# Recurrence halves in groups of four, and a gate moved from the weights to the projected result

## The chip, the cores and the metric

The kernel runs on one core of a Trainium2 chip, as one program. The metric is device time in microseconds of one execution. Three executions were timed, and a further one was taken by the hardware profiler; the rows below are from that one.

The engines are named as in the profile: PE is TensorE's matmul, PEld its weight load, DVE is VectorE, ACT ScalarE, POOL GpSimd, SP SyncE. PEclk is the granted clock of TensorE as a share of full speed.

## The reference, cut to what matters

One block of a mixed network on 1024 tokens of width 1024. What the change touches is the second branch (a gated linear recurrence), the merge of both branches, and the output projection with its residual gate `gt1`:

```python
def rglru_branch(xb, gb, conv_w, conv_b, w_rgate, b_rgate, w_igate, b_igate, lam):
    xc = conv(xb, conv_w) + conv_b                      # causal, width 4
    gate_r = sigmoid(blockdiag(xc, w_rgate) + b_rgate)
    gate_i = sigmoid(blockdiag(xc, w_igate) + b_igate)
    log_a = -8.0 * gate_r * softplus(-lam)
    a = exp(log_a)
    u = sqrt(-expm1(2.0 * log_a)) * (gate_i * xc)
    h = associative_scan(a, u)                          # h[t] = a[t] h[t-1] + u[t]
    return h * gelu(gb)
...
merged = (sigmoid(proj[..., o3:o4]) * (y_a @ p_a) + sigmoid(proj[..., o4:]) * (y_b @ p_b))
x = x + gt1[:, None, :] * (merged @ w_out)
h2 = modulate(rmsnorm(x, g_ffn), sh2, sc2)
x = x + gt2[:, None, :] * hier_moe(h2, ...)
```

`gt1` is one row of 1024 numbers, worked out from the condition `c`; it multiplies the columns of `merged @ w_out`.

## The kernel before, in words

The program is written once, without a loop on the device. A list scheduler sets the order on each engine when the program is built: among the instructions whose inputs and buffers it takes to be ready it issues the one that was written first. So a later line can be issued before an earlier one, but on the chip each engine then works through its list in order, and an instruction that waits holds up those behind it. SP issues nearly all DMAs, in one such list. Pools hand out buffers by name, with a fixed number each (`bufs`); a tile waits until the one that had its buffer is done with.

Products are made in pairs of a rounded value and its remainder: a weight `raw` is cast on ACT to `wh` (L216), the remainder `wl = raw - wh` is made on DVE (L217), and a product is `wh` by `yh`, `wh` by `yl` and `wl` by `yh`, three matmuls of 128 x 512 for each block of 128 inputs.

The stages around the change, in order of time in the profiled execution:

1. Up to 842.7 us: branch a and the projections into gates (`gd`), recurrence inputs (`xcd`, `ggd`) and branch a's result (`yad`), all in DRAM. The last store of `yad` is L643, the last gate halves are L769 and L770.
2. To 924.6: branch a's result is read in eight halves and split (L792 to L798, raw buffers of two). Then L878 to L880 run eight times: `lru(b, hf)` and `merge(0, n)`. `lru` takes one block `b` of 128 channels and half of the tokens: two gate matmuls (L833), two tanh on ACT (L834), exp (L837), tanh (L838) and sqrt (L839) on ACT, five operations and a scan (L844) on DVE, of which L840 needs the gates alone and the others the root; the result is cast on ACT (L849) and its remainder made on POOL (L850). The second half of a block takes the last column of the first. The scales of exp and tanh come from a short series on DVE in `lam` (L806 to L821). `merge(0, n)` multiplies branch a's result by a block of its weights: 24 matmuls in two PSUM banks of four, each then multiplied by its gate on DVE (L868). It does not use the recurrence's result.
3. To 989.2: `merge(1, d)` for eight blocks `d`, 24 matmuls each over the recurrence's result (`yh[4..7]`, `yl[4..7]`), DVE (L870), POOL (L871), ACT (L872) and DVE (L874) on each half. After each one, two pieces of the output weights of 128 x 512 are loaded, multiplied by `gt1` on POOL (L915), cast on ACT (L917) and their remainder made on DVE (L918): eight pieces of the first half of the output columns in the first four blocks, eight of the second half in the others.
4. From then to about 1107: the output projection, first the left half of the columns for eight tiles of 128 tokens (`hf == 0`, 24 matmuls a tile), then the right half. DVE adds each to `x1` (L1107), ACT squares it (L1108). In the right half each finished tile is transposed and multiplied by the router's weights, normalised and written to DRAM as `h2` (L1119 to L1126). The loads of `x` (L1072) and of three rows go out ahead of the first half, the first eight expert weights of 512 KB (`issue(8)`, L1095) with the second.

`x1` takes the place of `ybs`, in which the recurrence's result lies, so `x` is loaded once the last merges have read that. The output weights lie in 16 buffers `w` that the expert weights use after them.

Of the kernel before, what the change touches and what calls it, by code (L numbers as in the profile page):

```python
# [92 lines left out]
def _build(tc, A, out, dump, stop, top):  # L93
# [3 lines left out]
    def dmp(name, ap, idx=slice(None)):  # L97
        if name in dump:
            Y.dma_start(dump[name][idx], ap)
# [523 lines left out]
    def rwkv_finish(q):  # L623
        pd, hf, rk, yt = (q[n] for n in ("pd", "hf", "rk", "yt"))
        p, vs, g2 = pd["p"], pd["vs"], pd["g2"]
        tsl = slice(hf * 512, hf * 512 + 512)
        dmp("wkv", yt, (p, slice(None), tsl))

        yo = tmp.tile([128, 512], F32, name="u")
        S.activation(yo, yt, AF.Square)  # L630
        pss = psum.tile([128, 4, 2], F32, name="u1")
        for j in range(4):
            T.matmul(pss[:, j], yo[:, j * 128:j * 128 + 128], bo64[:, 0:128:64], start=True, stop=True)
        pin = inv_bcast(pss, GN_EPS)
        V.scalar_tensor_tensor(yt, yt, col("lnx_g", p), pin.rearrange("p j t -> p (j t)"), op0=OP.mult, op1=OP.mult)
        pb = psum.tile([128, 512], F32, name="u1")
        T.matmul(pb, bo, rk, start=True, stop=True)
        V.tensor_mul(rk, pb, vs[:, tsl])
        V.scalar_tensor_tensor(yo, yt, col("lnx_b", p), rk, op0=OP.add, op1=OP.add)
        pg = psum.tile([128, 512], F32, name="u2")  # L640
        T.matmul(pg, g2, sg[:, tsl], start=True, stop=True)
        V.tensor_mul(yo, yo, pg)
        Y.dma_start(yad[p][:, tsl], yo)  # L643
        dmp("y_a", yo, (p, slice(None), tsl))


# [174 lines left out]
    V.tensor_scalar(sp[:, 5], sp[:, 5], 2.0, None, op0=OP.mult)  # L821
    prev = {}

    def lru(b, hf):
        sl = slice(hf * 512, hf * 512 + 512)
        xc, gg = half("xc"), half("gg")
        Y.dma_start(xc, xcd[b][:, sl])
        Y.dma_start(gg, ggd[b][:, sl])
        dmp("xc", xc, (b, slice(None), sl))
        gr, gi = half("gr"), half("gi")  # L830
        for i, (dst, bias) in enumerate(((gr, "brh"), (gi, "bih"))):
            pg = psum.tile([128, 512], F32, name="pt", bufs=2)
            T.matmul(pg, wbd[:, b, i], xc, start=True, stop=True)  # L833
            S.activation(dst, pg, AF.Tanh, scale=0.5, bias=dcol[bias][:, b:b + 1])  # L834

        rc = half("rc")
        S.activation(rc, gr, AF.Exp, scale=sp[:, 0, b:b + 1], bias=sp[:, 0, b:b + 1])  # L837
        S.activation(gr, gr, AF.Tanh, scale=sp[:, 5, b:b + 1], bias=sp[:, 5, b:b + 1])  # L838
        S.activation(gr, gr, AF.Sqrt)  # L839
        V.scalar_tensor_tensor(gi, gi, 1.0, xc, op0=OP.add, op1=OP.mult)  # L840
        V.scalar_tensor_tensor(gr, rc, 1.0, gr, op0=OP.add, op1=OP.mult)
        V.tensor_mul(gr, gr, gi)
        hs_ = half("hs")
        V.tensor_tensor_scan(hs_, rc, gr, prev[b][:, 511:512] if hf else 0.0, op0=OP.mult, op1=OP.add)  # L844
        prev[b] = hs_
# [5 lines left out]


    def merge(i, d):
        raw = wpool.tile([128, 512], F32, name="wr", bufs=2)
        Y.dma_start(raw, A["pab"][i, d])
        wh, wl = split_w(raw, wpool)
        for hf in range(2):
# [17 lines left out]
                                       op1=OP.subtract)  # L875
                dmp("merged", g, (d, slice(None), sl))

    for n in range(8):  # L878
        lru(n // 2, n % 2)
        merge(0, n)  # L880
    gs_.close()
    yas.close()
    if stop == "lru":
# [18 lines left out]
    V.tensor_scalar(tri, rel, 0.0, None, op0=OP.is_gt)  # L902
    onb = rpc.tile([128, 128], BF, name="onb")
    V.memset(onb, 1.0)

    gt1 = wpool.tile([128, 1024], F32, name="gt1", bufs=1)
    load_row(gt1, 0)
    oh_, ol_ = {}, {}
    for d in range(8):
        merge(1, d)  # L910
        for kk in (2 * d, 2 * d + 1):
            hf, k = divmod(kk, 8)
            raw = wpool.tile([128, 512], F32, name="wo", bufs=2)
            Y.dma_start(raw, A["wout"][:, k, hf * 512:hf * 512 + 512])
            P.tensor_mul(raw, raw, gt1[:, hf * 512:hf * 512 + 512])  # L915
            h, l = (lambda t: (t[:, 0], t[:, 1]))(wo.tile([128, 2, 512], F32R, name="w", bufs=NRAW))
            S.copy(h, raw)  # L917
            V.tensor_sub(l, raw, h.bitcast(F32))  # L918
            oh_[k, hf], ol_[k, hf] = h, l
    m2.close()  # L920
    rp = rps.enter_context(pool("rp", 1, side="right"))
    if stop == "merged":
# [137 lines left out]
    with pool("xt", 1) as xt:  # L1060
        for i, n in enumerate(MODS[1:3]):
            mrow[n] = xt.tile([128, 1024], F32, name="m_" + n)
            load_row(mrow[n], i + 1)
        gf_ = xt.tile([128, 1024], F32, name="h2", bufs=2)
        Y.dma_start(gf_, A["grow"][0:1].to_broadcast([128, 1024]))
        V.scalar_tensor_tensor(mrow["sc2"], mrow["sc2"], 1.0, gf_, op0=OP.add, op1=OP.mult)
        for n in MODS[1:3]:
# [24 lines left out]
        for hf in range(2):  # L1092
            sl = slice(hf * 512, hf * 512 + 512)
            if hf:
                issue(8)  # L1095
            for t in range(8):
                tsl = slice(t * 128, t * 128 + 128)
                xv = x1[:, t]
# [4 lines left out]
                for k in range(8):  # L1103
                    T.matmul(ps, mh[k][:, tsl], oh_[k, hf], start=(k == 0), stop=False)
                    T.matmul(ps, mh[k][:, tsl], ol_[k, hf], start=False, stop=False)
                    T.matmul(ps, ml[k, t // 4][:, t % 4 * 128:t % 4 * 128 + 128], oh_[k, hf], start=False, stop=(k == 7))  # L1106
                V.tensor_add(xv[:, sl], xv[:, sl], ps)  # L1107
                S.activation(ps, xv[:, sl], AF.Square, accum_out=ssx[:, t, hf:hf + 1])  # L1108
                if hf == 0:
                    continue  # L1110
# [5 lines left out]
                pl2 = psum.tile([128, 36], F32, name="pl", bufs=2)  # L1116
                T.transpose(pl2, lgT, ident[0:36, 0:36])
                V.scalar_tensor_tensor(LG[:, t], pl2, y, br, op0=OP.mult, op1=OP.add)
                h2 = xt.tile([128, 1024], F32, name="h2", bufs=2)  # L1119
                if t == 7:  # L1120
                    choose(xt, 5, 8)
                for i in range(2):
# [371 lines left out]
```

## Time and profile before

| | us |
|---|---|
| median of 3 runs | 1537.52 |
| lowest and highest | 1531.68, 1541.69 |
| profiled execution, its own time | 1536.43 |
| its span, first to last instruction | 1534.5 |
| PE busy in the span | 1326.4 (86%) |
| DVE, ACT, POOL busy | 920.1, 490.3, 408.1 |
| mean granted TensorE clock | 0.945 |

Matmuls are pipelined and their ends are modelled, so two that follow at once overlap in the records, and the time that one takes off the engine is read from the distance of their starts. A number in brackets behind an instruction is the engine's idle time ahead of it, and who ended it. The chain of work that ended last is PE for 60% of the span and DVE for 20%.

### The profile page before, as it was taken

What the parts mean: (1) busy time and instruction counts of PE and PEld (TensorE: products, weight loads), DVE (VectorE), ACT (ScalarE), POOL (GpSimd) and SP (SyncE); (2) the same over time, 40 slices, a digit from 0 to 9 for tenths busy, and PEclk for the clock granted to TensorE, in tenths of its full rate; (3) what the DMA queues carried; (4) which work ended last, traced back from release to release, by engine and by line L of the source; (5) the groups of instructions that cost most, each with busy time, mean ns of one, the idle gap of its engine ahead of it and who ended that gap; (6) DMA issues with size and microseconds to landing.
All of it is one profiled execution on the core that took longest, in us unless ns stands there. A gap on an engine that the chain in (4) does not pass through costs nothing.

```text
span 1534.5 us, 23186 instructions
## 1 busy us (share of the span) xinstructions
PE 1326.4 (86%) x8524; PEld 926.5 (60%) x8524; DVE 920.1 (60%) x2073; ACT 490.3 (32%) x900; POOL 408.1 (27%) x327
## 2 busy tenths in 40 slices
PE   1898998899999999999999797899759899999910
PEld 0686765666766667766766475687545555755500
DVE  8936868687658562475433577614775435625557
ACT  3222323132222222231211693312424424514321
POOL 7001212121101110111111326601314434634514
PEclk9998999999999999999999899999969999999965
DMA  6333432333433211112211754541448979979952
GB/s 262 130 117 138 126 110 92 99 99 115 151 131 94 66 57 35 51 57 60 63 42 35 238 167 150 187 163 56 165 165 299 385 281 402 349 267 393 349 234 100
DMA packets 113403, 248.59 MB, mean 162 GB/s; under 512 B 39632, under 2 KB 40960, under 8 KB 112256
## 3 DMA queue, kind: packets, MB, share of 16 engines
q1 hardware_dynamic: 105952, 230.22, 42.7%
q0 software_dynamic: 7328, 16.79, 3.0%
q8 instruction: 69, 1.13, 0.3%
q14 instruction: 54, 0.44, 0.1%
HBM read 218.16 MB, written 38.36 MB: 167 GB/s over the span
## 4 chain that ended last, share of the span: by engine, by line
PE 60%; DVE 20%; DMA 9%; ACT 4%; issue 4%; POOL 2%; POOLq 0%; SPq 0%; DVEq 0%; ACTq 0%
PE pg L319 5%; PE pg L318 5%; PE pg L320 5%; DMA xg<-h2d,gidx 3%; DMA w<-in_we 3%; PE ph L1372 3%; PE pj L318 2%; DVE wa L228 2%; PE pj L320 2%; PE pj L319 2%; PE st L603 2%; PE ph L1315 2%; PE st L617 2%; PE pj L1106 2%; PE ph L1317 2%
## 5 line engine op out<-in xcount | busy, mean ns | idle before, releaser
L318 PE MATMUL pg<-hh,wh 128*128 128x512 f32 x376 | 158.9, 423 | 8.4 <-DVE cr L680 5.0
L319 PE MATMUL pg<-hl,wh 128*128 128x512 f32 x376 | 157.2, 418 | 0.0
L320 PE MATMUL pg<-hh,wl 128*128 128x512 f32 x376 | 155.9, 415 | 0.0
L560 POOL TENSOR_TENSOR WV<-VT,m 128x512 f32<-128x512 f32 x32 | 35.5, 1110 | 369.5 <-PE st L603 280.3
L1282 ACT CAST wh<-w 128x1024 fp32r<-128x1024 f32 x96 | 98.5, 1053 | 82.1 <-DMA w<-in_we 30.7
L1283 DVE TENSOR_TENSOR wl<-w,wh 128x1024 fp32r<-128x1024 f32 x68 | 92.0, 1376 | 36.1 <-ACT wh L1282 33.7
L228 DVE SCALAR_TENSOR_TENSOR wa<-wa,cb 128x1024 f32<-128x1024 f32 x64 | 79.6, 1251 | 27.1 <-DMA wa<-in_wada 27.0
L318 PEld LDWEIGHTS pg<-hh,wh 128*128 128x128 f32 x376 | 72.3, 192 | 33.3 <-issue 9.4
L216 ACT CAST wh<-wr 128x512 fp32r<-128x512 f32 x88 | 54.4, 619 | 100.0 <-PE pj L319 50.4
L217 DVE TENSOR_TENSOR wl<-wr,wh 128x512 fp32r<-128x512 f32 x72 | 53.5, 742 | 50.7 <-ACT wh L216 50.4
L319 PEld LDWEIGHTS pg<-hl,wh 128*128 128x128 f32 x376 | 72.3, 192 | 17.7 <-issue 4.7
L320 PEld LDWEIGHTS pg<-hh,wl 128*128 128x128 f32 x376 | 71.9, 191 | 17.2 <-issue 4.0
L610 DVE SCALAR_TENSOR_TENSOR St<-St,Dc,st 128x64 f32<-128x64 f32 x128 | 35.4, 277 | 76.4 <-PE st L608 76.3
L318 PE MATMUL pj<-hh,wh 128*128 128x512 f32 x192 | 77.5, 404 | 3.2 <-DVE carry L365 3.2
L1283 POOL TENSOR_TENSOR wl<-w,wh 128x1024 fp32r<-128x1024 f32 x28 | 71.0, 2541 | 30.6 <-ACT wh L1282 23.1
L320 PE MATMUL pj<-hh,wl 128*128 128x512 f32 x192 | 76.9, 401 | 0.0
L319 PE MATMUL pj<-hl,wh 128*128 128x512 f32 x192 | 75.8, 395 | 0.0
L1315 PE MATMUL ph<-wh,th 128*128 128x512 f32 (+4 forms) x160 | 65.4, 409 | 7.1 <-ACT th L1304 6.8
L515 DVE TENSOR_TENSOR X<-X,UC 128x60 f32<-128x60 f32 (+24 forms) x248 | 65.9, 266 | 4.2
L1372 PE MATMUL ph<-w,th 128*64 128x512 f32 x256 | 65.7, 598 | 1.8 <-ACT th L1363 1.7
L513 DVE TENSOR_TENSOR UC<-X,Ui 128x60 f32<-128x60 f32 (+24 forms) x248 | 63.3, 255 | 4.4
L1317 PE MATMUL ph<-wh,tl 128*128 128x512 f32 (+4 forms) x160 | 63.9, 399 | 1.9 <-DVE tl L1305 1.9
(503 smaller groups left out, 3139.0 us busy)
## 6 DMA issues: line engine op xcount, KB each, us to landing
w<-in_we SPq DMA_DIRECT2D x192, 512.0 KB
wa<-in_wada SPq DMA_DIRECT2D x64, 512.0 KB
wr<-in_win SPq DMA_DIRECT2D x72, 256.0 KB
gd<-gt SPq DMA_DIRECT2D x32, 256.0 KB
g<-gd SPq DMA_DIRECT2D x32, 256.0 KB
yy<-yd SPq DMA_DIRECT2D x8, 1024.0 KB
xT<-in_xT SPq DMA_DIRECT2D x8, 512.0 KB
Ui<-Ud SPq DMA_DIRECT2D x32, 128.0 KB
```

The costliest lines, as they stand in the source:

```text
L216: S.copy(h[:, :n], raw)
L228: V.scalar_tensor_tensor(wa, wa, 1.0, cb, op0=OP.mult, op1=OP.mult, accum_out=ccol[:, i:i + 1])
L318: T.matmul(ps, wh[:, o:o + 128], hh[k][:, sl], start=(k == 0), stop=False)
L319: T.matmul(ps, wh[:, o:o + 128], hl[k][:, sl], start=False, stop=False)
L320: T.matmul(ps, wl[:, o:o + 128], hh[k][:, sl], start=False, stop=(k == n - 1))
L513: V.tensor_mul(t_, X[:, :nj, s:s + 1].to_broadcast([128, nj, nt]), Ui[:, s, None, s + 1:32].to_broadcast([128, nj, nt]))
L515: V.tensor_add(X[:, :nj, s + 1:32], X[:, :nj, s + 1:32], t_)
L1282: S.copy(h, raw)
L1283: (P if pool_engine else V).tensor_sub(l, raw, h.bitcast(F32))
L1315: T.matmul(ph[R], th[:, k, R], h[:, o:o + 512], start=(k == 0), stop=False)
L1317: T.matmul(ph[R], tl[:, k, R], h[:, o:o + 512], start=False, stop=(k == 7))
L1372: T.matmul(ph[C], tp[:, k, C], W[s_][k // 2][:, o:o + 512], start=(k == 0), stop=(k == 7))
```

## The change

- `lru` is cut into `gates` (up to the tanh ahead of the root, and L840) and `recur` (from L841 on). The eight halves are taken in two groups of four. A group's four `gates` come first, then two merges of branch a, then the four roots together, then four `recur`, then two more merges. The roots are queued on ACT behind the group's last gate, the second group's gates on ACT behind the first group's last root. `xc`, `gr` and `rc` have four buffers each instead of two; L840 writes into `xc`.
- `gt1` no longer multiplies the output weights; the projected result is multiplied by it on DVE in PSUM, in both halves of the columns, ahead of L1107. It is loaded in halves inside the projection's loop instead of whole ahead of the merges.
- Output weights: with `merge(1, d)` only the piece `(d, left half)` is loaded and split; the piece `(t, right half)` is loaded and split in tile `t` of the projection's left half, through one raw buffer.
- `merge`'s raw weights have four buffers instead of two, `h2` one instead of two.
- The last store of `yad` goes out on ACT's queue.

```diff
-        Y.dma_start(yad[p][:, tsl], yo)
+        (S if p == 3 and hf == 1 else Y).dma_start(yad[p][:, tsl], yo)
...
-    def lru(b, hf):
+    marks = {}
+
+    def gates(b, hf):
         sl = slice(hf * 512, hf * 512 + 512)
-        xc, gg = half("xc"), half("gg")
+        xc = half("xc", 4)
         Y.dma_start(xc, xcd[b][:, sl])
-        Y.dma_start(gg, ggd[b][:, sl])
-        dmp("xc", xc, (b, slice(None), sl))
-        gr, gi = half("gr"), half("gi")
+        gr, gi, rc = half("gr", 4), half("gi"), half("rc", 4)
         for i, (dst, bias) in enumerate(((gr, "brh"), (gi, "bih"))):
             pg = psum.tile([128, 512], F32, name="pt", bufs=2)
             T.matmul(pg, wbd[:, b, i], xc, start=True, stop=True)
             S.activation(dst, pg, AF.Tanh, scale=0.5, bias=dcol[bias][:, b:b + 1])
-
-        rc = half("rc")
+        V.scalar_tensor_tensor(xc, gi, 1.0, xc, op0=OP.add, op1=OP.mult)
+
         S.activation(rc, gr, AF.Exp, scale=sp[:, 0, b:b + 1], bias=sp[:, 0, b:b + 1])
-        S.activation(gr, gr, AF.Tanh, scale=sp[:, 5, b:b + 1], bias=sp[:, 5, b:b + 1])
-        S.activation(gr, gr, AF.Sqrt)
-        V.scalar_tensor_tensor(gi, gi, 1.0, xc, op0=OP.add, op1=OP.mult)
+        marks["g"] = S.activation(gr, gr, AF.Tanh, scale=sp[:, 5, b:b + 1], bias=sp[:, 5, b:b + 1])
+        return xc, gr, rc
+
+    def recur(b, hf, xc, gr, rc):
+        sl = slice(hf * 512, hf * 512 + 512)
+        gg = half("gg")
+        Y.dma_start(gg, ggd[b][:, sl])
         V.scalar_tensor_tensor(gr, rc, 1.0, gr, op0=OP.add, op1=OP.mult)
-        V.tensor_mul(gr, gr, gi)
+        V.tensor_mul(gr, gr, xc)
...
-        raw = wpool.tile([128, 512], F32, name="wr", bufs=2)
+        raw = wpool.tile([128, 512], F32, name="wr", bufs=4)
...
-    for n in range(8):
-        lru(n // 2, n % 2)
-        merge(0, n)
+    for B in range(2):
+        todo = [(b, hf) for b in (2 * B, 2 * B + 1) for hf in range(2)]
+        with ExitStack() as behind:
+            if B:
+                behind.enter_context(tc.issue_after(marks["r"].ins))
+            got = [gates(b, hf) for b, hf in todo]
+        merge(0, 4 * B)
+        merge(0, 4 * B + 1)
+        with tc.issue_after(marks["g"].ins):
+            for _, gr, _ in got:
+                marks["r"] = S.activation(gr, gr, AF.Sqrt)
+        for (b, hf), g in zip(todo, got):
+            recur(b, hf, *g)
+        merge(0, 4 * B + 2)
+        merge(0, 4 * B + 3)
...
-    gt1 = wpool.tile([128, 1024], F32, name="gt1", bufs=1)
-    load_row(gt1, 0)
     oh_, ol_ = {}, {}
+
+    def wout(hf, k, pl, bufs):
+        raw = pl.tile([128, 512], F32, name="wo", bufs=bufs)
+        w = wo.tile([128, 2, 512], F32R, name="w", bufs=NRAW)
+        Y.dma_start(raw, A["wout"][:, k, hf * 512:hf * 512 + 512])
+        S.copy(w[:, 0], raw)
+        V.tensor_sub(w[:, 1], raw, w[:, 0].bitcast(F32))
+        oh_[k, hf], ol_[k, hf] = w[:, 0], w[:, 1]
+
     for d in range(8):
         merge(1, d)
-        for kk in (2 * d, 2 * d + 1):
...
+        wout(0, d, wpool, 2)
...
+            gt1 = xt.tile([128, 512], F32, name="gt1")
+            Y.dma_start(gt1, md[4 * hf:4 * hf + 4].rearrange("(o a) b -> o (a b)", o=1).to_broadcast([128, 512]))
             for t in range(8):
...
+                V.tensor_mul(ps, ps, gt1)
                 V.tensor_add(xv[:, sl], xv[:, sl], ps)
+                if hf == 0:
+                    wout(1, t, xt, 1)
                 S.activation(ps, xv[:, sl], AF.Square, accum_out=ssx[:, t, hf:hf + 1])
...
-                h2 = xt.tile([128, 1024], F32, name="h2", bufs=2)
+                h2 = xt.tile([128, 1024], F32, name="h2", bufs=1)
```

## Rows read from the trace of the kernel before

**Rows 1.** Stretch, us; busy us of PE, PEld, DVE, ACT, POOL (records); clock, DMA, GB/s:

```profile
842.70:870.00 27.30, 16.41 (x51) 9.44 (x50) 12.78 (x39) 13.16 (x20) 9.64 (x8) 0.75 0.75 227
870.00:924.60 54.60, 54.60 (x218) 40.38 (x216) 42.42 (x57) 47.98 (x63) 14.74 (x11) 1.00 0.57 187
924.60:933.20 8.60, 4.37 (x11) 3.14 (x11) 5.69 (x9) 2.80 (x5) 5.02 (x7) 0.80 0.30 112
933.20:989.20 56.00, 46.10 (x181) 34.68 (x179) 42.00 (x46) 19.48 (x32) 40.18 (x28) 0.94 0.47 151
```

**Rows 2.** First stretch, L833 alone, and L1079 from the timeline:

```profile
842.70:870.00 27.30, 5.11 (x8) 2.05 (x8) 0.75 0.75 227
...
842.73 1.87 PE L1079 MATMUL pl<-wr__7814,ccol 128*128 128x36 f32 x16
```

**Rows 3.** TensorE in order of time (start us, us), a step of the full stretch:

```profile
904.10 1.88 PE L833 MATMUL pt<-xc,wbd 128*128 128x512 f32 x4
...
906.04 0.40 PE L863 MATMUL pj<-yl,wh 128*128 128x512 f32 x1
...
911.08 0.39 PE L864 MATMUL pj<-yh,wl 128*128 128x512 f32 x1
```

**Rows 4.** ScalarE in order of time, gates and root of one step:

```profile
901.48 0.69 ACT L834 ACTIVATE gr<-pt,der 128x512 f32<-128x512 f32 x1
...
902.64 0.82 ACT L837 ACTIVATE rc<-gr,sp 128x512 f32<-128x512 f32 x1
...
906.32 0.64 ACT L839 ACTIVATE gr<-gr 128x512 f32<-128x512 f32 x1
```

**Rows 5.** Groups by line, 858 to 925 us (count, busy us, mean ns):

```profile
L839 ACT ACT_TABLE_LOAD x8 | 10.3, 1283 | 0.1
```

**Rows 6.** End of the recurrence in order of time, idle time and its releaser in brackets:

```profile
923.56 1.28 DVE L844 TENSOR_TENSOR_SCAN hs<-rc,hs,gr 128x512 f32<-128x512 f32 x1
...
925.34 0.69 DVE L847 SCALAR_TENSOR_TENSOR gg<-hs,gg 128x512 f32<-128x512 f32 x1
...
927.71 0.60 ACT L849 CAST x<-gg 128x512 fp32r<-128x512 f32 x1
...
928.37 0.50 PE L862 MATMUL pj<-x,wh 128*128 128x512 f32 x1 [3.61 <-ACT x L849]
...
928.39 1.27 POOL L850 TENSOR_TENSOR x<-gg,x 128x512 fp32r<-128x512 f32 x1 [1.25 <-ACT x L849]
```

**Rows 7.** Before the recurrence in order of time, DMA queue and ScalarE:

```profile
844.45 0.38 SPq L758 DMA_DIRECT2D gt<-md  x1
...
851.19 0.62 ACT L797 CAST yh<-wr 128x512 fp32r<-128x512 f32 x1 [3.33 <-DMA wr<-yad]
```

**Rows 8.** Waits, 929 to 989 us (us in total, times, longest us):

```profile
PE pj L864 <- DVE wl L217: 6.1, 4, 2.6
```

**Rows 9.** Two lines' instructions (ns min/median/max, first and last start us):

```profile
L918 DVE TENSOR_TENSOR w<-wo,w x16: 676/1536/1779, 931.6 to 991.4; 128x512 fp32r<-128x512 f32 x16
...
L915 POOL TENSOR_TENSOR wo<-wo,gt x16: 1270/1513/1793, 874.9 to 988.5; 128x512 f32<-128x512 f32 x16
```

**Rows 10.** TensorE in order of time, turn of the projection's halves:

```profile
1027.41 0.39 PE L1106 MATMUL pj<-w,ml 128*128 128x512 f32 x1
...
1034.30 0.39 PE L1105 MATMUL pj<-w,mh 128*128 128x512 f32 x1
```

**Rows 11.** Busy us by stretch, once x is loaded:

```profile
1003.00:1006.00 3.00, 3.00 (x15) 2.49 (x14) 0.00 (x0) 0.00 (x0) 0.00 (x0) 1.00 0.03 14
```

**Rows 12.** A load of 256 KB and the cast that waited for it:

```profile
853.22 1.55 SPq L796 DMA_DIRECT2D wr<-yad  x2
...
855.72 0.62 ACT L797 CAST yh<-wr 128x512 fp32r<-128x512 f32 x1 [2.92 <-DMA wr<-yad]
```

**Rows 13.** Store of a tile of h2, and the next tile's first write:

```profile
1100.33 0.33 SPq L1126 DMA_DIRECT2D h2d<-h  x1
...
1104.49 0.75 DVE L1124 SCALAR_TENSOR_TENSOR h<-x,rq,m_sc 128x512 f32<-128x512 f32 x1
```

More of the change, by code (lines that the diff above doesn't have):

```diff
@@ L904, in _build @@
     V.memset(onb, 1.0)
-    gt1 = wpool.tile([128, 1024], F32, name="gt1", bufs=1)
-    load_row(gt1, 0)
     oh_, ol_ = {}, {}
+    def wout(hf, k, pl, bufs):
[5 more added lines that the diff above has]
+        oh_[k, hf], ol_[k, hf] = w[:, 0], w[:, 1]
     for d in range(8):
         merge(1, d)
-        for kk in (2 * d, 2 * d + 1):
[L912 to L919, printed above, removed]
+        wout(0, d, wpool, 2)
     m2.close()
@@ L1063, in _build @@
             load_row(mrow[n], i + 1)
-        gf_ = xt.tile([128, 1024], F32, name="h2", bufs=2)
+        gf_ = xt.tile([128, 1024], F32, name="h2", bufs=1)
         Y.dma_start(gf_, A["grow"][0:1].to_broadcast([128, 1024]))
```

## The prediction

> **What bounds the kernel now.** I read the page's slices first, then split the stretch that the edits touch into stages and asked each engine's busy time per stage, then the waits of the stages where TensorE (PE) is not full. [rows 1] are the four stretches from the last gate matmul of the front (842.7 us) to the point from which PE runs without a gap (989.2). The reader is to see that the second, 870.0 to 924.6, is full: PE is busy 54.60 of 54.60 us. So eight times "one step of the recurrence and one merge of branch a" costs what PE needs, and not what ScalarE (ACT) needs, though ACT is busy 47.98 of it, with a change of function table before each root and another after it. The pitch of one matmul is (911.08 - 906.04)/22 = 0.229 us, and the four records of the two gate matmuls (L833) take 906.04 - 904.10 - 0.229 = 1.71 [rows 3]. A step is 24 x 0.229 + 1.71 = 7.2 us.
>
> What PE loses, as span less records times pitch:
> - 842.7 to 870.0: 51 records, of them 16 small ones of the routing bias (L1079, 1.87 us together) and 8 of L833, which is two gate steps [rows 1, 2]. Work 1.9 + 2 x 1.71 + 27 x 0.229 = 11.5; lost 15.8. Its cause: the first yad halves land only at 851.19 [rows 7], and the clock is 0.75 on the mean.
> - 870.0 to 924.6: 24 of L833 and 194 others, 54.7; lost 0.
> - 924.6 to 933.2: 11 records, 2.5; lost 6.1. PE waits 3.61 us for the copy of the last recurrence half, which itself starts 1.7 us after its input is ready (925.34 + 0.69 to 927.71), then for the subtraction on GpSimd (POOL), and runs on at half clock (0.80 on the mean) [rows 1, 6].
> - 933.2 to 989.2, merges of branch b: 181 records, 41.4; lost 14.6. The named wait is wl, VectorE's (DVE) remainder of the next weights [rows 8]; behind it stand the two remainders of output weights per step (median 1.54 us, 0.68 at best), which wait for casts, which wait for the gate product on POOL (1.51 each, 16 of them) [rows 9].
>
> Together 36.5 us lost; the edits can hardly bring more, since the matmuls stay the same.
>
> **The change part by part.** Lines are those of the kernel before.
>
> *Tables.* Roots in two groups leave two of the eight loads ahead of the roots [rows 5], and as many fewer on the way back: 12 x 1.28 = 15.4 us off ACT. In the full stretch PE sets the pace, so this alone is worth nothing there.
>
> *Grouping (L824 to L880).* What it can win is the front and the tail. Front: four gate steps (4 x 1.71 = 6.8 us of PE) come ahead of the merges and need only xc and wbd, so PE has work while yad is read. The 512 KB load of gt1 at 844.45, ahead of the yad reads on SyncE's (SP) queue, is gone [rows 7]; 0.5 MB at the 227 GB/s of this stretch is 2.3 us [rows 1]. The last yad store goes to ACT's queue, and SP no longer waits for it with the weight, yad and xc loads behind; on ACT only the tanh of the last gate half stands behind it, which needs later matmuls anyway. The exps still wait for the lam series on DVE, and half clock stays for part. I take 5 us, bounds 2 (only the load) and 8 (half of what is lost).
>
> Tail: the groups form a chain. A half's gates take ACT 1.16 + 0.82 + about 0.82 = 2.8 us, four of them 11.2; a group of roots 1.28 + 4 x 0.64 = 3.8 [rows 4]; a half's recurrence takes DVE 1.28 + 3 x 0.69 = 3.35, four 13.4; then a copy of 0.60 and POOL's 1.27 [rows 6]. Taking 857 for the first gates (the first cast of yad, 851.19 [rows 7], and the lam series come before), roots are done at 872, first recurrences 872 to 889 with merge steps between, and as each frees xc, gr and rc, the gates of the second group follow, up to about 898 when PE's earlier merges go first; roots 902, recurrences until 916, last remainder 918. PE, 5 us ahead of now, ends the merges of branch a at about 913.5 and asks for the last half some 4 us later. So 6.1 lost becomes about 3: gain 3, bounds 6 (no wait) and -3 (no overlap of groups: last remainder about 931).
>
> *Merges of branch b.* POOL loses 16 x 1.51 us, DVE 8 of 16 remainders, SP 8 loads, and wr has four buffers, so that its load no longer stands behind wo loads. DVE's step is then four operations of 0.69 (as in [rows 6]) and two remainders, wl's and wo's, of 0.68 to 1.54 each: 4.1 to 5.8 us, against PE's 24 x 0.229 = 5.5. I take a loss of 4.6 instead of 14.6: gain 10, bounds 7 and 13.
>
> The spread 0.68 to 1.54 of one and the same operation [rows 9] is at the worse end while POOL multiplies. The Trainium skill, "SBUF — State Buffer", section "Who interferes with whom", says that a VectorE instruction with two SBUF inputs contends with a GpSimd instruction that reads SBUF, and that the one which comes second waits it out in full. By that rule the remainders cost little over 0.68 once POOL no longer multiplies, and the gain is 13; by the median row DVE is 0.3 us over PE in each of eight steps, and the gain is about 8. The spread in the trace agrees with the rule.
>
> *First half of the projection (L1092 to L1110).* Take M = 1027.41 + 0.23 - 192 x 0.229 = 983.7 as its start without gaps [rows 10]. gt1 is now loaded behind the eight x loads and three rows, which keep the DMA busy until 1003, M + 19 [rows 11]; they can start some 2 us earlier when no wo load stands ahead, and DVE's product waits for gt1 until about M + 18. Four PSUM banks let PE go on until M + 4 x 5.5 = M + 22, which hides it; past that it costs what the load is late. The extra product is 0.69 per tile of 5.5: hidden. Eight splits of wout follow through one raw buffer: a round is a load of 2.5 (853.22 to 855.72 [rows 12]), a cast of 0.60, a remainder of 0.68 and an allowance of 0.3, 4.1; with waits behind a tile's product and sum on DVE's queue (half of 1.38 on the mean) 4.8. First remainder at about M + 20, eighth at M + 20 + 7r; PE wants it at 1034.30 = M + 50.6. Loss 7r - 30.6: none at r = 4.1, 3 at 4.8, 11 at 6. I take 3, bounds 0 and 11. SP's queue has nothing else due then but the first expert loads.
>
> *Second half.* One more product ahead of each sum; PE has the next tile's matmuls between, so only the last tile shows it: 0.7. h2 with one buffer: the store goes out at 1100.33 and the next write comes at 1104.49 [rows 13], 4.2 us against a load's 2.5: 0, bounds 0 and 3. If late, the logits behind it on DVE wait too, and the routing.
>
> Sum: -5 - 3 - 10 + 3 + 0.7 = -14.3 us. Against the profiled execution (1536.43, of which the span is 1534.5) that gives 1522.1; the median of three is 1537.52, 1.1 above it, and half of that added gives 1522.6, which I say.
>
> **The rivals.**
> A. *PE is full everywhere:* rounds hide and the tail wait goes: -8 - 6 - 13 + 0.7 = -26, 1510. For it: ACT gets 15 us of room, and each added operation sits beside a full PE. Against: the clock at the front.
>
> B. *The grouped chain takes the place of the old tail:* recurrence groups do not overlap, front -2, tail +3, merges -8, the losses +3.7: -3.3, 1533. For it: xc, gr and rc have four buffers for eight halves, so the second group waits for the first by construction, and DVE is busy 42 of 54.6 already [rows 1]. Against: the buffers come free one at a time, the first three recurrences (10 us) ahead of the last.
>
> C. *Slower: the single raw buffer paces the turn of the halves.* With 17.3 us gained elsewhere (18 less 0.7) it decides from 7r - 30.6 = 17.3, r = 6.8. Eleven loads of 512 KB between M and 1003 make 1.7 us each; if two expert loads of that size get in front of each round, r is 4.8 + 3.4 = 8.2, the loss 27 and the time 1546; at r = 9.2 it passes 1552. For it: PE cannot pass the eighth weights. Against: expert slots come free only with the last tile, when most rounds are over.
> Best Practices in "Trainium Kernel Development and Optimization" (the Trainium skill) asks to double-buffer so that transfers overlap with compute; wo and h2 go the other way, which is this rival.
>
> D. *The edits move no bound:* table loads come off an ACT that isn't the bound, and DVE paces the merges as now (5.8 and waits). The 14.6 us lost in a stage with POOL's product in it speak against, so I give it little.
>
> **How the numbers follow.** Forecast case (-20 to -9) 0.50; A 0.17; B 0.20; C 0.08; D 0.05 (1536 or so). The range leaves out C and half of A, and with B's and D's scatter some 0.2: 1510 to 1538. About 1% (15.4 us, so 1522.1 and 1552.9 around the median) is what a measurement here can tell from no change. Faster by more than that: A and half of the forecast, 0.17 + 0.25 = 0.42. Slower by more: the long end of C, 0.04. The rest 0.54.
>
> **What would show it.** In the new profile: the root's table load twice; PE full from about 855 to the end of the merges; the wait for the last recurrence half under 3 us; no wait for wl over 1 us; merge step of branch b at 5.5 to 6.1; the eighth remainder of wout's second half before PE asks. The forecast is wrong if PE idles between the groups of gates, if gt1 lands after M + 22, or if the rounds are longer than 5 us.

## The result, and the profile after

| | before | after |
|---|---|---|
| median, us | 1535.99 of 7 runs | 1548.38 of 7 runs |
| lowest and highest | 1531.14, 1547.08 | 1541.02, 1552.58 |
| profiled execution, its own time | 1536.43 | 1541.02 |
| its span | 1534.5 | 1539.2 |

The ratio is 1.0058, 95% interval 1.0034 to 1.0082: the change makes the kernel 0.6% slower. 1522.6 was predicted, with 1538 as the upper end. The kernel before was timed again beside the changed one, so its median differs a little from the one given at the start. The profiled execution of the changed kernel is the fastest of its seven: the two profiles differ by 4.6 us, the medians by 12.4, and what follows accounts for the two profiles alone.

Lines L8xx to L13xx are now those of the kernel after: `gates` L826 to L838, roots L892, `recur` L845 to L854, `merge` L866 to L878, output weights L926 to L928, projection L1121 to L1125.

The busy time of the engines in the same four stretches as [rows 1]:

```profile
core 0: us, PE busy (x) PEld busy (x) DVE busy (x) ACT busy (x) POOL busy (x), PEclk, DMA share, GB/s
842.70:870.00 27.30, 17.90 (x52) 9.36 (x51) 10.26 (x36) 11.96 (x20) 8.82 (x8) 0.75 0.72 217
870.00:924.60 54.60, 41.12 (x151) 28.48 (x151) 44.94 (x54) 31.83 (x48) 12.93 (x9) 0.92 0.46 152
924.60:933.20 8.60, 8.60 (x29) 6.83 (x29) 3.03 (x7) 1.24 (x2) 1.90 (x5) 0.72 0.44 153
933.20:989.20 56.00, 52.75 (x221) 40.83 (x220) 31.09 (x45) 16.70 (x29) 20.07 (x14) 1.00 0.40 132
```

The second stretch, in which PE was full (54.60 of 54.60), now has 13.5 us of holes; the fourth has fewer than before. The waits of PE from 870 to 929 us name what ended the holes (us in total, times, longest):

```profile
PE pj L868 <- DVE wl L217: 7.3, 1, 7.3
PE pj L866 <- DVE ml L872: 5.6, 2, 4.3
```

Both are DVE's own. Its list in order of time, at the first group's recurrences and at the end of the second's:

```profile
881.49 1.22 DVE L848 TENSOR_TENSOR_SCAN hs<-rc,gr 128x512 f32<-128x512 f32 x1
...
883.81 1.28 DVE L848 TENSOR_TENSOR_SCAN hs<-rc,hs,gr 128x512 f32<-128x512 f32 x1
...
887.22 1.21 DVE L848 TENSOR_TENSOR_SCAN hs<-rc,gr 128x512 f32<-128x512 f32 x1
888.36 1.68 DVE L845 SCALAR_TENSOR_TENSOR gr<-rc,gr 128x512 f32<-128x512 f32 x1
889.96 0.68 DVE L872 SCALAR_TENSOR_TENSOR ml<-g,pj 128x512 f32<-128x512 f32 x1
...
891.76 1.27 DVE L848 TENSOR_TENSOR_SCAN hs<-rc,hs,gr 128x512 f32<-128x512 f32 x1
...
921.29 1.27 DVE L848 TENSOR_TENSOR_SCAN hs<-rc,hs,gr 128x512 f32<-128x512 f32 x1
922.49 1.68 DVE L217 TENSOR_TENSOR wl<-wr,wh 128x512 fp32r<-128x512 f32 x1
```

And PE's matmuls that waited behind them:

```profile
884.63 1.88 PE L833 MATMUL pt<-xc,wbd 128*128 128x512 f32 x4
890.78 0.47 PE L866 MATMUL pj<-yh,wh 128*128 128x512 f32 x1 [4.28 <-DVE ml L872]
...
916.57 0.40 PE L867 MATMUL pj<-yl,wh 128*128 128x512 f32 x1
924.22 0.79 PE L868 MATMUL pj<-yh,wl 128*128 128x512 f32 x1 [7.26 <-DVE wl L217]
```

The recurrences stand one behind the other on DVE: from 879.08 to 889.96 nothing else is between, and the fourth scan comes at 891.76. The merges' gate products (L872), which free the PSUM banks, and the next weights' remainder (L217), without which a merge stops at its third matmul, come behind them. At 916.6 PE has done what it can and waits until 924.2 for the wl of 922.49.

Where the 4.7 us of span come from, by landmarks that both traces have:

| stretch | before | after | difference |
|---|---|---|---|
| first matmul of branch b's merges at | 918.51 | 935.84 | +17.3 |
| from there to the projection's first matmul | 63.7 | 49.8 | -13.9 |
| projection, left half, on PE | 45.4 | 46.4 | +1.0 |
| from there to the last sum | 73.7 | 75.3 | +1.6 |
| to the first expert's matmul | 37.6 | 37.1 | -0.4 |
| the rest | | | -0.9 |

Of the 13.9, 6.1 is the wait for the last recurrence half, which the prediction counted by itself ([rows 1], third stretch). PE is so late that this half is long done; so the grouping's own balance is +17.3 - 6.1 = +11.2, and the merges of branch b gain 7.8. The +17.3 itself is for the most part the 13.5 us of holes; by the estimate in the last section, some 4 us more went to the lower clock of PE behind them.

### The profile page after: what moved, and what is told of

The parts are those of the page before. It is cut to its first block, busy times and chain, and to the rows that moved or that the text cites. A ratio compares the mean times of both kernels' runs of the same rounds, so it can differ in the third digit from the quotient of the medians.

```text
span 1539.2 us, 23179 instructions
## 1 busy us (share of the span) xinstructions
PE 1330.0 (86%) x8524; PEld 926.3 (60%) x8524; DVE 923.1 (60%) x2089; ACT 474.7 (31%) x890; POOL 381.3 (25%) x311
## 4 chain that ended last, share of the span: by engine, by line
PE 60%; DVE 20%; DMA 9%; issue 5%; ACT 3%; POOL 2%; POOLq 0%; SPq 0%; DVEq 0%; ACTq 0%
PE pg L319 5%; PE pg L318 5%; PE pg L320 5%; DMA xg<-h2d,gidx 3%; PE ph L1392 3%; PE pj L318 2%; PE pj L320 2%; PE pj L319 2%; DVE wa L228 2%; PE st L603 2%; PE st L617 2%; PE ph L1335 2%; PE ph L1337 2%; DMA w<-in_we 2%; PE ph L1336 2%
## 5 line engine op out<-in xcount | busy, mean ns | idle before, releaser
L217 DVE TENSOR_TENSOR wl<-wr,wh 128x512 fp32r<-128x512 f32 x72 | 53.1, 739 | 47.7 <-ACT wh L216 47.4
L1335 PE MATMUL ph<-wh,th 128*128 128x512 f32 (+4 forms) x160 | 65.9, 412 | 7.0 <-ACT th L1324 7.0
L513 DVE TENSOR_TENSOR UC<-X,Ui 128x60 f32<-128x60 f32 (+24 forms) x248 | 63.7, 257 | 4.4
```

The lines of the kernel that those rows point to most:

```text
L513: V.tensor_mul(t_, X[:, :nj, s:s + 1].to_broadcast([128, nj, nt]), Ui[:, s, None, s + 1:32].to_broadcast([128, nj, nt]))
L1335: T.matmul(ph[R], th[:, k, R], h[:, o:o + 512], start=(k == 0), stop=False)
```

## Experiments

Theory **Q** at the start: a group's recurrences stand ahead of its last two merges on DVE. Rival **W**: the late split and gt1 at the projection cost the time. Rival **G**, later sharpened to **L**: the groups' chain itself, in whatever order, leaves DVE too little time. The front of the traces shifts by some us from run to run (the first gate matmul, L833, comes between 852.3 and 860.4 us in the runs compared here), so stretches are counted from that matmul to the first one of branch b's merges and to the first one of the projection. They are from one trace of each kernel. All ratios are to the kernel before.

| kernel | to branch b, us | to projection, us | ratio | 95% interval |
|---|---|---|---|---|
| before | 59.8 | 123.5 | 1 | |
| after | 77.2 | 127.0 | 1.0058 | 1.0034 to 1.0082 |
| e1_ungrouped | 60.3 | 113.8 | 0.9952 | 0.9938 to 0.9966 |
| e2_grouping_alone | 78.6 | 140.4 | 1.0093 | 1.0075 to 1.0111 |
| e3_merges_ahead | 66.1 | 121.8 | 1.0009 | 0.9988 to 1.0029 |
| e4_alternating | 65.9 | 119.0 | 1.0006 | 0.9983 to 1.0028 |
| e6_all_splits_early | 59.8 | 117.3 | 0.9955 | 0.9937 to 0.9974 |
| e7_shared_half_buffers | 60.6 | 113.6 | 0.9937 | 0.9912 to 0.9962 |
| e8_gate_on_pool | 59.9 | 117.1 | 0.9981 | 0.9960 to 1.0002 |
| e9_groups_of_two | 66.1 | 119.7 | 0.9988 | 0.9969 to 1.0007 |
| e10_gate_on_result_only | 60.3 | 119.4 | 0.9965 | 0.9940 to 0.9990 |
| e13_changed_w3 | 74.4 (see below) | 120.9 | 1.0030 | 1.0007 to 1.0052 |
| e14_alternating_w3 | 65.2 | 118.7 | 1.0009 | 0.9993 to 1.0026 |

**Which part costs.** e1 takes the grouping out of the change, e2 puts it alone into the kernel before. The edit of e1, shortened (e2 is the reverse of it):

```diff
-    for B in range(2): ... gates x4, merge x2, roots x4, recur x4, merge x2
+    for n in range(8):
+        lru(n // 2, n % 2)
+        merge(0, n)
```

> The changed kernel with the grouping alone undone: one half's gates, root and recurrence and one merge of branch a in turn, as in the kernel before; gt1 on the result, late output weights, the buffers and the yad store stay as changed. Theory Q (the recurrences of a group stand ahead of two merges on VectorE's queue, and TensorE starves): the first matmul of branch b's merges comes at about 918.5 again instead of 935.8, the merges of branch b keep the changed kernel's step of about 6, so the projection starts at about 973 (985.6 in the changed kernel), 10 to 13 us off the changed kernel, ratio to the kernel before 0.994 to 0.999. Theory W (the weights' split and gt1 at the projection cost the time): the projection takes longer by what was lost and the ratio stays at 1.004 to 1.008.

> The kernel before with the grouping alone (gates, roots and recurrences in groups of four, with their four buffers); gt1 on the weights, all sixteen splits with branch b's merges, as before. Theory Q: branch b's merges start on TensorE at about 935, and keep the old pace (57 us without the old wait for the last recurrence), so the projection starts at about 993 against 982.2, ratio 1.005 to 1.011. Theory W: the grouping costs nothing, ratio 0.997 to 1.001.

Branch b's first merge is back at 60.3 in e1 and goes to 78.6 in e2, with the same two waits of PE as after (7.3 us for wl, 4.3 for the bank). The ratios, -0.5% and +0.9%, add up to about that of the whole change. Q holds against W; the projection started later in e2 than expected (1000.8 against 993), for the merges of branch b took 61.8 us there and not 57, with 9.4 us of waits for wl and wh. The other edits, which are e1, gain: 1529.3 us of median against 1536.5.

**Order or groups.** e3 and e4 keep the groups and move only the merges in the text (shortened):

```diff
 e3:  gates x4, merge, merge, roots x4
+     merge, merge
      recur x4
-     merge, merge
 e4:  gates x4, roots x4, then four times: merge, recur
```

> The changed kernel with the last two merges of each group written ahead of that group's four recurrences, so that they come first on VectorE; the groups and their roots stay. Theory Q (queue order): TensorE runs the merges of branch a without holes and ends them at about 916 to 920, then waits for the last recurrence half until about 928; the projection starts at about 973 to 977, ratio 0.996 to 1.000. Theory G (the chain of the groups itself: gates, roots, recurrences one after the other, whatever the order on VectorE): the last recurrence half and branch b's merges come no earlier than in the changed kernel, 926 to 936, TensorE is idle elsewhere, and the ratio stays at 1.004 or above.

> The changed kernel with the merges of a group written alternately with its recurrences, each merge ahead of one recurrence; groups and roots stay. Theory Q: as with all merges ahead, branch a ends at 916 to 922, the last recurrence half at about 925, the projection starts at 971 to 976, ratio 0.994 to 0.999. Theory G: ratio 1.004 or above, the last remainder not before 926.

Both give back about half of what the grouping costs, 0.5 of 1.1%, where Q wanted nearly all: the order was part of the cause, not all of it. The ratios lie between what Q and G had each expected.

> The changed kernel with groups of two halves instead of four (four groups: two gates, two roots together, then merge, recurrence, merge, recurrence). Theory L (in groups of four the first scan comes at 881 instead of 868, so that VectorE has eight recurrences left for a stretch in which it also serves the merges): the first scan comes at 871 to 875, the scans come in pairs, branch a ends at 918 to 921, ratio 0.996 to 0.999, between the ungrouped 0.995 and the alternating groups of four 1.001. If only the order of merges and recurrences on VectorE matters, groups of two equal alternating groups of four, 1.000 to 1.002.

```diff
 e9:  four times: gates x2, roots x2, merge, recur, merge, recur
```

Groups of two start their first scan at 873.0, but the rest is as in e4 (66.1, 119.7), and the intervals of the ratios overlap: this told nothing apart. Branch a ended at 923, not at the 918 to 921 that L expected. PE still waits 3.7 us there for a wl that stands behind a scan, so the next two runs give wh and wl a third buffer (`split_w(raw, wpool, 3)`, and three raw buffers for room).

> The changed kernel, groups and order kept, with three buffers instead of two for wh and wl of the merges (and three for the raw weights, for room), so that the next weights' remainder can be made before a group's four recurrences. Theory B (the remainder's buffer): the wait for wl of 7.3 us at the end of branch a falls under 3, but that for the free PSUM bank (4.3 us) stays; the first merge of branch b comes 70 to 74 us behind the first gate instead of 77.2, ratio 1.000 to 1.004. Theory L (VectorE has too little time left): the wait moves to the bank or to the recurrence, 76 us or more, ratio 1.004 to 1.008.

> Groups of four with merges and recurrences alternating (as e4_alternating), with three buffers for wh and wl (and three for the raw weights). Theory B: branch b's first merge comes 60 to 62 us behind the first gate instead of 65.9, as in the ungrouped kernel (60.3), ratio 0.994 to 0.997. Theory L: 65 or more, ratio 0.999 to 1.002.

In e13 four matmuls of branch b slip in ahead of the end of branch a, at 63.2 us from the first gate:

```profile
922.49 0.76 PE L866 MATMUL pj<-x,wh 128*128 128x512 f32 x1 [3.89 <-DVE ml L872]
...
933.43 0.39 PE L868 MATMUL pj<-yh,wl 128*128 128x512 f32 x1
933.66 0.40 PE L868 MATMUL pj<-x,wl 128*128 128x512 f32 x1
```

Its merges of branch b run on only behind the last matmul of branch a, at 74.4 us, which is what compares with the others: 2.8 us less than after, just above the 70 to 74 expected with the buffer as the cause and below the 76 expected of L. The wait for wl falls from 7.3 to 0.9 us, but that for the bank grows from 5.6 to 8.8. The ratio falls from 1.0058 to 1.0030, and the intervals overlap. In e14 PE waits for wl even longer than in e4 (7.7 us against 2.1) and nothing is won. So the buffer is worth a small part at most, and not the other half. What the alternating order still has is seen in the windows of e4:

```profile
858.00:878.00 20.00, 19.33 (x59) 11.08 (x59) 5.90 (x9) 16.72 (x26) 5.54 (x5) 0.90 0.74 241
878.00:890.00 12.00, 10.78 (x44) 7.96 (x43) 12.00 (x16) 6.04 (x10) 3.10 (x2) 1.00 0.52 160
890.00:900.00 10.00, 7.36 (x23) 3.79 (x23) 8.98 (x12) 6.15 (x11) 3.73 (x2) 1.00 0.65 196
900.00:910.00 10.00, 10.00 (x44) 7.98 (x43) 6.61 (x10) 8.02 (x12) 0.00 (x0) 1.00 0.31 98
910.00:925.00 15.00, 13.65 (x59) 10.41 (x58) 15.00 (x20) 3.48 (x7) 4.46 (x3) 1.00 0.45 142
```

The third number pair is DVE: 12.00 of 12.00 and 15.00 of 15.00 in the bursts, 5.90 of 20 and 6.61 of 10 while a group's gates are made. PE's longest wait in e4 is put down to ACT:

```profile
897.44 1.12 PE L833 MATMUL pt<-xc,wbd 128*128 128x512 f32 x2 [2.64 <-ACT gi L834]
```

But ACT had stood still, behind a cast whose input DVE had not made, and the tanh came next in its list:

```profile
896.18 0.62 ACT L853 CAST x<-gg 128x512 fp32r<-128x512 f32 x1 [2.78 <-DVE gg L851]
896.70 0.68 ACT L834 ACTIVATE gi<-pt,der 128x512 f32<-128x512 f32 x1
```

With the 2.1 us for wl, 4.7 of the 5.9 us for which PE stands still in e4 between the first gate and branch b's merges go back to DVE's burst; in e1 PE stands still for 1.5 us there in all. The ungrouped kernel has the same work spread evenly, with PE full:

```profile
870.00:918.00 48.00, 47.88 (x188) 35.03 (x188) 37.28 (x53) 45.24 (x60) 10.77 (x9) 1.00 0.62 200
```

So L: DVE is at 78% on the mean, and grouping makes it idle and then short. The last two runs take one DVE operation of each recurrence half (L845) out of both orders, which changes the output, so that the traces are read up to the projection alone:

> e4_alternating without the first VectorE operation of each recurrence half (the product with rc plus one, L845 of the changed kernel, eight times 0.68 us), which changes the output; read in the trace up to the projection alone, as the routing changes behind it. Theory L (VectorE is the bound within the bursts): branch b's first merge comes 2.5 to 5.5 us earlier than 65.9 behind the first gate, the projection starts at 114 to 117 behind it instead of 119.0. Rival (ScalarE's or the loads' order sets the holes): 65 to 66 and 118 to 120.

> e1_ungrouped without the same operation, eight times. Theory L: VectorE has room there, so branch b's first merge stays at 60.3 behind the first gate within 0.7, and the projection start moves from 113.8 by the 0.7 us of the last half's chain at most.

(One execution each.) Alternating: 65.9 to 63.4 and 119.0 to 115.6. Ungrouped: 60.3 to 60.4 and 113.8 to 113.1. The same operations are worth 3.4 us in one order and 0.7 in the other, as L has it. Of the 5.2 us between the two orders (119.0 against 113.8) about half is thereby shown by an edit; for the other half L's account rests on the waits of e4 above, as DVE is still full from 878 to 890 us in that run.

**Are the table loads worth anything?** e12 replaces the root by tanh in e1:

```diff
-        S.activation(gr, gr, AF.Sqrt)
+        S.activation(gr, gr, AF.Tanh)
```

> Beside e1_ungrouped: the root is replaced by tanh, which changes the recurrence's input and so the output, so that ScalarE needs no table load between gates and root; the operations and their shapes stay. This takes away all 15 loads of the stretch (19 us of ScalarE) with no grouping. If the loads are worth nothing where TensorE is full (the prediction's term of 0): branch a ends within 1 us of 918.3 and the wait for the last recurrence half falls by at most 2.6 us, projection start 969.5 to 972.5. If ScalarE's loads pace the recurrence, branch a ends at 913 or earlier and the projection starts before 968. The whole time is read with care, as the routing of the tokens changes with the output.

ACT's busy time falls from 45.24 of 48 us to this, with no table load left:

```profile
870.00:913.00 43.00, 43.00 (x168) 31.37 (x167) 36.78 (x49) 27.99 (x42) 7.78 (x6) 1.00 0.62 199
```

PE is full in both. Absolute times look like a gain (branch b at 913.95, projection at 966.7, which by itself is in the rival's range of before 968), but the whole front is earlier in this execution: from the first gate it is 61.6 us to branch b (60.3 with the loads) and 114.4 to the projection (113.8). The wait for the last recurrence half, 2.1 us in e1, is gone, and nothing came of it. 15 loads of 1.28 us were worth nothing that this trace shows: the two distances are longer by 1.3 and 0.6 us, not shorter. (Its total, 1557.6 us, is that of other tokens at other experts.)

**What brings the gain in branch b's merges.** e10 is the kernel before with the gate moved to the result and nothing else; e6 is e1 with all sixteen splits at the merges; e8 is e1 with the product of the eight early pieces back on POOL, and none on the left half's result:

```diff
 e6: -        wout(0, d, wpool, 2)
     +        for kk in (2 * d, 2 * d + 1):
     +            wout(*divmod(kk, 8), wpool, 2)
     ...
     -                if hf == 0:
     -                    wout(1, t, xt, 1)
 e8: +        if hf == 0:
     +            P.tensor_mul(raw, raw, gw)
     ...
```

> Beside e1_ungrouped: all sixteen pieces of the output weights are loaded and split with branch b's merges, as in the kernel before, with gt1 on the result, so GpSimd has no product there. Theory P (GpSimd's product is what stretched VectorE's remainders and held up the weights): a remainder stays at 0.69 us in the median, the merges of branch b stay within 2 us of e1's (projection start 972 to 975), ratio 0.994 to 0.997. Theory N (the number of remainders on VectorE): the projection starts at 977 or later, remainders or not, ratio 0.998 or above.

> Beside e1_ungrouped: the eight pieces of the left half are multiplied by gt1 on GpSimd again, as in the kernel before, ahead of their cast; the right half stays late with gt1 on the result. Theory P: remainders in this stage take about 1.5 us again in the median of the eight early ones, the projection starts 4 to 8 us later than 972.5, ratio 0.998 to 1.000. Theory N: eight splits fit with or without the product, the projection starts within 2 us of e1's, ratio 0.994 to 0.996.

> The kernel before with one thing changed: gt1 multiplies the projected result on VectorE instead of the weights on GpSimd, all sixteen splits with branch b's merges (h2 has one buffer, for the room of gt1). Theory P: the remainders fall to 0.69 us in the median, the projection starts at 972 to 975, ratio 0.994 to 0.997, the same as with the late splits, the yad store on ScalarE's queue and four weight buffers, which are then worth nothing by themselves. If those other edits matter, the ratio is 0.998 or above.

e6 has the ratio of e1: sixteen splits cost 3.5 us more in the merges (117.3 against 113.8) and give it back in the projection, whose last sum comes 120.1 us behind its start and not 123.1. So the late split is worth nothing that the ratio shows. With the product back on POOL, 3.3 of e1's 9.7 us up to the projection are gone; with the gate alone moved, 4.1 of them are there. Of the 3.3, 1.9 is a longer wait for the last recurrence half (4.0 us against 2.1); the waits for wl are nearly the same (2.3 against 2.1). So in e8 POOL's product did not cost by starving PE of wl, which is what the prediction held against it. From the kernel before to e10 both waits fall, that for wl from 6.1 to 4.2 and that for the half from 3.6 to 2.2. The eight early remainders of e8 take 1.22 us in the median, not the 1.5 expected, and the sixteen of e6 0.69. P holds in the ratios of both; the projection of e8 starts 3.1 us behind e1's (975.6 against 972.5), between N's limit of 2 and P's 4 to 8. The expected absolute starts of e10 were met (973.5) only because its front was early, and its ratio alone says that most of the gain is the gate's.

**The front, the single buffers.**

```diff
 e5:  -  raw = half("wr")                     +  raw = half("wr", 4)           (reads of yad)
 e7:  -  h2 of 128 x 1024 in one buffer, wo in one
      +  three buffers of 128 x 512 for both, h2 stored in halves
```

> Beside e1_ungrouped (grouping undone, the rest as changed): the eight halves of branch a's result are read through four raw buffers instead of two. Theory F (the two raw buffers pace the front: the third read waits for the first cast and holds up the weights and gate inputs behind it on SyncE): the first gate step comes some 4 us earlier than 858.7, branch a's last matmul at 914 to 916 instead of 918.3, and the time falls by 2 to 4 us, ratio 0.992 to 0.994. Rival (the half clock and the pair of casts on ScalarE and GpSimd pace it): branch a ends at 917.5 to 918.5 and the ratio stays at 0.995.

> Beside e1_ungrouped: the late raw output weights and h2 share three buffers of half a row (128 x 512), so that neither goes through a single buffer; h2 is stored in two halves. If the single raw buffer or the single h2 buffer costs time, as the prediction's term of 3 us for the turn has it, the time falls by 1 to 4 us, ratio 0.992 to 0.994. If both are hidden, as the changed kernel's trace reads (no wait of TensorE at the turn over 0.3 us), the ratio stays at 0.995 within 0.002.

> The ungrouped kernel with the three shared half buffers (0.994 before) and four raw buffers for branch a's result together: the candidate for the fastest. If both help a little, ratio 0.991 to 0.993; if the first was the only one, 0.993 to 0.995.

> Ungrouped, with the three shared half buffers (as e7_shared_half_buffers) and four buffers for wh and wl of the merges. TensorE waits for wl only 1.4 us and for wh 0.6 us in all in branch b's merges without them: gain 0 to 2 us, ratio 0.992 to 0.994. If it is nothing or lost to order on VectorE, 0.994 or above.

e5: 0.9963 (0.9939 to 0.9987). Branch a ends 1.8 us earlier (its last matmul starts at 916.99, in e1 at 918.76), the first gate comes later (863.8, behind merges), and two new waits of PE in branch b's merges (1.2 and 1.5 us, at 935 to 937) take it back. So the cause that F names (the two raw buffers of the reads) is there, but not its gain. In e7 PE has no wait left at the turn of the halves, where e1 has one of 0.2 us, so the trace gives the single buffers little to cost; e7 has the lowest ratio, e11 0.9947 (0.9925 to 0.9969), e15 0.9946 (0.9926 to 0.9966); none of the three can be told from e1. All beat the kernel before, e7 with 1526.5 us of median.

## Why the prediction was wrong, point by point

*The step that failed is the tail under "Grouping".* It says "first recurrences 872 to 889 with merge steps between" and lets PE end branch a at about 913.5; the last matmul of branch a started at 935.6. It followed the recurrence's chain and asked only when its result is ready. That chain came out late (roots done at 880.0 and 908.9 against 872 and 902, last remainder at 926.8 against 918), but PE, later still, never waited for it. What the step never asked is who stands behind the recurrences on DVE: banks and weights of the merges that were to fill PE meanwhile. Written behind the `recur`s, they had lower rank in the list. So PE lost 7.3 us to a wl and 5.6 to a bank that were due behind a recurrence, which no term of the sum had, nor the lower clock behind each hole. By e3 and e4 the order is half of it; the other half is that grouping leaves DVE short of time in its bursts (L). Front and tail together were put at -8 and measured +11.2; the two other terms of some us came out inside their bounds. (One reading was off without effect: PE asks for the last half 6.2 us into branch b's merges, from 918.51 to 924.76 in the kernel before, and not some 4.)

*Rival B* had the right engine (DVE busy 42 of 54.6 us), but its condition holds only in part: the second group's first gate matmul starts at 884.63, while the first group's last scan starts at 891.76. Its price for the tail is +3, as it too saw only the lateness of the last half. *Rival A* falls with the holes of PE, *rival D* with e1, which is 0.5% faster.

*Front, -5.* Measured -0.6 (first merge at 851.28, before 851.87). The gates were meant to run while yad is read; but their loads stand behind yad's third read on SP, which waits for a raw buffer:

```profile
846.99 0.61 SPq L802 DMA_DIRECT2D wbd<-in_wg  x1
852.61 1.55 SPq L796 DMA_DIRECT2D wr<-yad  x2
854.21 1.37 SPq L829 DMA_DIRECT2D xc<-xcd  x3
```

So the first gate matmul starts at 858.67, before 858.76. The first cast came 0.6 us earlier too ([rows 7]: 851.19, now 850.61), but no run separates the load of gt1, which is gone, from the scatter of the front. The prediction saw the queue and not this wait.

*Tables, 0.* Right, as far as e12 shows.

*Merges of branch b, -10 (bounds 7 to 13).* 7.8 measured, near the 8 that the prediction drew from remainders of 1.54 us; as they became shorter than that, the nearness is luck. Remainders of output weights, against [rows 9]:

```profile
L928 DVE TENSOR_TENSOR w<-wo,w x16: 679/691/1785, 937.2 to 1038.3; 128x512 fp32r<-128x512 f32 x16
```

The median fell from 1536 to 691 ns. "SBUF — State Buffer" (the Trainium skill), section "Who interferes with whom", as the prediction used it, agrees with the runs: between 930 and 975 us in the kernels before, after, e1, e6 and e8, all 36 remainders on DVE (wl and w) that took over 1 us had begun 0.4 to 1.1 us after an operation of POOL that was still running, and ended 0.55 us after it. One pair of e8, DVE and POOL in order of time:

```profile
935.53 1.78 DVE L217 TENSOR_TENSOR wl<-wr,wh 128x512 fp32r<-128x512 f32 x1
```
```profile
935.08 1.68 POOL L871 TENSOR_TENSOR g<-g,ml 128x512 f32<-128x512 f32 x1 [1.23 <-DVE g L870]
```

26 others overlapped an operation of POOL too, but had begun 0.16 to 0.23 us before it, and took 0.68 to 0.69 us, like the 18 that overlapped none. So which of the two begins first decides it. The 13 us that the prediction drew from the rule did not come: POOL keeps its other operation of the merges (L875), behind which three remainders of the changed kernel still took 1.79 us, and of the 5.8 us still lost, waits for wl (2.1) and wh (1.2) remain.

*First half of the projection, +3.* +1.0, and most of that is not the term: PE's one wait there is for the last merge (1.9 us; before, 0.9 and 0.4). The chain of the right half's weights came as worked out: gt1 landed 19.1 us behind the start (18 was said, 22 the limit), the first remainder at +20.9 (20), seven rounds of 4.53 on the mean (4.8). The eighth came when PE asked:

```profile
1039.00 0.51 PE L1122 MATMUL pj<-w,mh 128*128 128x512 f32 x1 [0.23 <-DVE w L928]
```

*Rival C* is thereby refused, with r = 4.5 and not 8.2. The expert loads come after the last round on SP's queue.

*Second half, +0.7.* +1.6; DVE shows no wait for h2's single buffer.

*The signs.* Of those named, there came the two root loads, no wait for the last recurrence half, and no wait for wl over 0.7 us in branch b's merges (their step is 49.8/8 = 6.2, just over the 6.1 said). In branch a's there was one of 7.3, and PE was not full. Of those that were to prove the forecast wrong, one came: PE idles between the groups. The root's loads, in the groups by line:

```profile
L892 ACT ACT_TABLE_LOAD x2 | 2.6, 1283 | 0.0
```

## What to carry to other kernels

Work that is grouped to save one engine something comes as a burst on the next: before grouping, take the engine that gets the burst (here DVE, 78% beside a full PE), add up what else it must deliver during the burst, and see who waits for that. In an in-order list, ask of each moved step not only when its own result comes, but which results of others now stand behind it: a PSUM bank that isn't freed and a weight that isn't split stop the engine that was full. And a saving on an engine beside a full one (19 us of table loads here) should be priced at zero until a run without them says otherwise.

## What the runs showed of the hardware that was not expected

With a table load ahead of each root and one behind it ACT lost only their 1.28 us each (in the kernel before an activation ends at 905.00, the load runs from 905.02 to 906.30, the root starts at 906.32), and PE beside it stayed full with ACT at 94% (45.24 of 48) as with 65% (27.99 of 43).

PE's holes in the changed kernel came with a lower clock, which stayed low for some us of work behind them; in the kernel before, the same stretch of branch a has 1.00 with PE full ([rows 1]). The granted clock was 0.50 of full speed, the lower level of 1.2 GHz, from 892 to 895 us behind the hole of 4.3, and from 920 to 929 us in and behind the hole of 7.3:

```profile
892.00:895.00 3.00, 3.00 (x5) 1.29 (x4) 3.00 (x4) 2.80 (x5) 1.53 (x1) 0.50 0.43 156
...
924.30:929.00 4.70, 4.70 (x11) 3.72 (x12) 1.46 (x5) 0.62 (x1) 1.90 (x5) 0.50 0.62 222
930.00:935.00 5.00, 5.00 (x24) 4.14 (x23) 1.98 (x3) 0.62 (x1) 0.00 (x0) 1.00 0.48 151
```

Matmuls started 0.43 us apart in the second of these stretches (924.82, 925.24, 925.67) and 0.23 in the third (929.49, 929.72, 929.95). PE worked about 3.4 and 5.2 us at the lower level, so by estimate from these distances some 4 us went to the clock: a hole cost more than its length.
